# Nearest-neighbour upsampling: the second and third load issued behind the opening barrier and eight drains

## The chip, the cores and the metric

The kernel runs on one core of one Trainium2 chip. The metric is the device time of one execution in microseconds (us); of several executions, the median counts.

A core has five engines, each with its own queue of instructions: TensorE (PE), VectorE (DVE), ScalarE (ACT), GpSimd (POOL) and SyncE (SP). Data moves between the chip's main memory and the core's on-chip memory through 16 DMA engines. An engine that issues a transfer only hands it over, and goes on to its next instruction; the transfer itself runs on the DMA engines, and counts up a semaphore when it has landed.

## The reference

The input x has the shape (16, 64, 64, 64) in float32, 16.78 MB. Each element is written four times, so that height and width double; the output has the shape (16, 64, 128, 128), 67.11 MB.

```
for i in range(new_h):
    for j in range(new_w):
        src_i = i // scale_factor
        src_j = j // scale_factor
        result[:, :, i, j] = x[:, :, src_i, src_j].copy()
```

The scale factor is 2. There is no arithmetic: the kernel moves and repeats data.

## The kernel before, in words

**Tiling.** All rows of the input (16 x 64 x 64 of them, 64 elements each) are laid over the 128 partitions, 512 consecutive rows for each. So a partition's input is one run of 128 KB in main memory, and its output one run of 512 KB. The whole input fits on chip: one large on-chip tile holds it in `xt`, with free room ahead of it (lines 188 to 190).

**Loads.** Three loads bring the input in, cut by rows of a partition at `cuts = [0, 32, 288, 512]` (lines 194 to 197): the first has 32 rows (8 KB for each partition, 1 MB in all), the second 256 (64 KB, 8.4 MB), the third 224 (56 KB, 7.3 MB). All three are issued on SyncE's queue.

**Copies and stores.** The loop at line 206 goes over nine groups of rows, `[54, 38, 54, 60, 54, 62, 64, 62, 64]`. For each, VectorE copies the rows into their expanded form, every element twice and every row twice (line 217), and one store sends that to main memory (line 219). The expanded groups lie by turns in the free room ahead of `xt` and over input rows that have been used up. Group 0 is copied in two parts: its first row (line 216), which is in the first load, and its other 53 rows (line 217), which reach into the second load and wait for it. The stores 0, 1 and 8 are issued by SyncE, the others by ScalarE.

**What sets the order at the start.** The program has a first block, which ends in a barrier of all five engines, and a second block, the body, reached by a branch. In the barrier each engine executes a drain that counts up a gathering semaphore; GpSimd waits for all of them and then counts up the releasing semaphore, for which each engine waits. The barrier's instructions carry line 237 in the profile, the branch and the closing barrier line 251.

The loads stand in the body as it is built. `begin_before_barrier` (line 13) changes the finished program: it takes the first `EARLY` instructions of SyncE's body, which must be loads that wait for nothing, and puts them into the first block, ahead of SyncE's drain of the barrier. With `EARLY = 3` SyncE's queue therefore begins: load 1, load 2, load 3, drain, wait for the release, branch, and then the stores.

`close_early` (line 80) does something like it at the end, where GpSimd cleans up while the last store is in flight and SyncE waits for that store alone. The change doesn't touch it.

Of the kernel before, what the change touches and what calls it, by code (L numbers as in the profile page):

```python
# [6 lines left out]

EARLY = 3  # L10


def begin_before_barrier(nc):
# [5 lines left out]
    sp = mybir.EngineType.SP  # L19
    loads = [i for i in body.instructions if i.engine == sp][:EARLY]  # L20
    for load in loads:
# [132 lines left out]
@with_exitstack  # L154
def kernel(
    ctx: ExitStack,
    tc: tile.TileContext,
    x: bass.AP,
    scale_factor: int,
    out: bass.AP,  # L160
):
    nc = tc.nc
    nc.at_finalize(begin_before_barrier)
    nc.at_finalize(close_early)
    P = nc.NUM_PARTITIONS
    s = int(scale_factor)
    B, C, H, W = x.shape
    R = B * C * H // P
    fdt = x.dtype

    xp = x.rearrange("b c h w -> (b c h) w").rearrange("(p r) w -> p r w", p=P)
    op = out.rearrange("b c (h hd) w -> (b c h) (hd w)", hd=s).rearrange(
        "(p r) w -> p r w", p=P
    )

    rows = [54, 38, 54, 60, 54, 62, 64, 62, 64]
    GROW = s * s
    FREE = 79
    WF = FREE * GROW * W
    assert sum(rows) == R
    mem_pool = ctx.enter_context(tc.tile_pool(name="mem", bufs=1))
    LEAD = 32
    whole = mem_pool.tile([P, LEAD + WF + R * W], fdt, name="mem")
    mem = whole[:, LEAD:]
    xt = mem[:, WF:].rearrange("p (r w) -> p r w", r=R)  # L190

    HEAD = 32
    cuts = [0, HEAD, R // 2 + HEAD, R]
    for lo, hi in zip(cuts, cuts[1:]):
        nc.sync.dma_start(out=xt[:, lo:hi], in_=xp[:, lo:hi])  # L197

    def expanded(r0, r1):
        return (  # L200
            xt[:, r0:r1].unsqueeze(2).unsqueeze(4).to_broadcast([P, r1 - r0, s, W, s])
        )

    r0 = 0
    before = (0, 0)
    for n, k in enumerate(rows):
        size = k * GROW * W
        at = 0 if n % 2 == 0 else WF + r0 * W - size
        assert at >= before[1] or at + size <= before[0]
        before = (at, at + size)  # L210
        u = mem[:, at : at + size].rearrange(
            "p (k a w b) -> p k a w b", k=k, a=s, w=W
        )
        k0 = 1 if n == 0 else 0
        if k0:
            nc.vector.tensor_copy(out=u[:, :k0], in_=expanded(r0, r0 + k0))  # L216
        nc.vector.tensor_copy(out=u[:, k0:], in_=expanded(r0 + k0, r0 + k))  # L217
        issuer = nc.sync if n in (0, 1, len(rows) - 1) else nc.scalar
        issuer.dma_start(out=op[:, r0 : r0 + k, :], in_=u)
        r0 += k  # L220
# [35 lines left out]
```

## Time and profile before

| | |
|---|---|
| median of 3 runs | 197.26 us (197.02 to 197.47) |
| span of the profiled execution, first to last instruction | 195.8 us |
| what the median has beyond that span | 1.5 us |
| transfers | 12: 3 loads, 9 stores; 83.89 MB |
| mean rate over the span | 429 GB/s |
| VectorE busy | 76.9 us, 10 copies |

The page gives no time of the profiled execution beside its span; other executions of the kernel take the times of the first row.

How to read it: a profile's span runs from the first instruction to the last. Busy time is what an engine spends executing; register, branch, semaphore and transfer-issuing instructions don't count as busy. The "chain that ended last" follows the last piece of work back to what released it, step by step. "SPq" or "ACTq" in front of an operation means that the engine's queue issued or executed it without the engine counting as busy. The DMA row gives the mean busy share of the 16 DMA engines in 40 equal slices of a window, in tenths, with 9 for 90% or more. A packet is one run of bytes that one DMA engine moves; a transfer over 128 partitions has 128 of them here, and 16 small ones at its end that count up the semaphore. A packet's bytes are booked at one moment, so that short windows can show a rate or a share that is too high or too low.

### The profile page before, as it was taken

The numbers are of one execution on the slowest core, as the hardware profiler recorded it, in microseconds if no ns is written. First come the engines' busy times: TensorE is split into PE (matmuls) and PEld (weight loads), VectorE is DVE, ScalarE is ACT, GpSimd is POOL, SyncE is SP. The second block draws the span as 40 slices with busy tenths as digits, with TensorE's granted clock in tenths as the row PEclk, the third lists the DMA queues.
The fourth block names the chain that finished last, engine by engine and source line by source line (L and its number), as shares of the span: only waits on it lengthen the run. The fifth ranks groups of instructions, "written<-read, shape, count | busy, mean of one in ns | idle before, by whom it ended". The sixth has DMA issues, their size and how long they took to land.

```text
span 195.8 us, 76 instructions
## 1 busy us (share of the span) xinstructions
DVE 76.9 (39%) x10; POOL 0.2 (0%) x4
## 2 busy tenths in 40 slices
DVE  0000099990029287059008805920790079000000
POOL 0000000000000000000000000000000000000000
DMA  9999989989898988999999899999999999999994
GB/s 429 429 429 429 402 375 539 398 362 542 362 435 382 551 373 362 542 402 402 402 537 407 362 542 415 415 415 415 429 429 429 429 415 558 473 435 422 429 429 214
DMA packets 1728, 83.89 MB, mean 429 GB/s; under 512 B 192, under 2 KB 192, under 8 KB 192
## 3 DMA queue, kind: packets, MB, share of 16 engines
q10 hardware_dynamic: 864, 46.66, 55.0%
q1 hardware_dynamic: 864, 37.22, 44.2%
HBM read 16.78 MB, written 67.11 MB: 429 GB/s over the span
## 4 chain that ended last, share of the span: by engine, by line
DMA 61%; DVE 24%; SPq 0%; issue 0%
DMA out_dram<-mem 49%; DVE mem L217 24%; DMA mem<-in_x_dram 12%; SPq L197 0%
## 5 line engine op out<-in xcount | busy, mean ns | idle before, releaser
L217 DVE COPY mem<-mem 128x13824 f32<-128x13824 f32 (+5 forms) x9 | 76.6, 8515 | 84.6 <-DMA out_dram<-mem 65.6
L216 DVE COPY mem<-mem 128x256 f32<-128x256 f32 x1 | 0.3, 293 | 4.8 <-DMA mem<-in_x_dram 4.8
L237 POOL MEMSET const-bfloat16-1.0<- 128x1 bf16 x1 | 0.1, 102 | 0.0
L237 POOL MEMSET const-uint8-127<- 128x1 uint8 x1 | 0.1, 101 | 0.0
L237 POOL MEMSET const-float32-0.0<- 128x1 f32 x1 | 0.1, 98 | 0.2 <-issue 0.2
L237 POOL MEMSET const-float32-1.0<- 128x1 f32 x1 | 0.1, 98 | 0.0
## 6 DMA issues: line engine op xcount, KB each, us to landing
out_dram<-mem ACTq DMA_DIRECT2D x2, 7936.0 KB, 31.6
out_dram<-mem ACTq DMA_DIRECT2D x2, 6912.0 KB, 23.7
out_dram<-mem ACTq DMA_DIRECT2D x1, 7680.0 KB, 26.1
mem<-in_x_dram SPq DMA_DIRECT2D x1, 7168.0 KB, 40.2
out_dram<-mem SPq DMA_DIRECT2D x1, 6912.0 KB, 19.0
out_dram<-mem SPq DMA_DIRECT2D x1, 4864.0 KB, 25.2
mem<-in_x_dram SPq DMA_DIRECT2D x1, 1024.0 KB, 4.8
mem<-in_x_dram SPq DMA_DIRECT2D x1, 23.7
```

The source lines that it names most:

```text
L216: nc.vector.tensor_copy(out=u[:, :k0], in_=expanded(r0, r0 + k0))
L217: nc.vector.tensor_copy(out=u[:, k0:], in_=expanded(r0 + k0, r0 + k))
L237: nc = _bacc.Bacc("TRN2", target_bir_lowering=False, num_devices=1)
```

## The change

`EARLY` goes from 3 to 1, so that only the first load is put ahead of the barrier. In front of the second load SyncE gets eight drains that wait for nothing. SyncE's queue then begins: load 1, drain of the barrier, wait for the release, branch, eight drains, load 2, load 3, and then the stores as before. Copies, stores, their order and their engines stay as they are, and so do the sizes of the loads.

```diff
-EARLY = 3
+EARLY = 1
+PAUSES = 8
...
     cuts = [0, HEAD, R // 2 + HEAD, R]
-    for lo, hi in zip(cuts, cuts[1:]):
+    for n, (lo, hi) in enumerate(zip(cuts, cuts[1:])):
+        if n == 1:
+            for _ in range(PAUSES):
+                nc.sync.drain()
         nc.sync.dma_start(out=xt[:, lo:hi], in_=xp[:, lo:hi])
```

## The prediction

> **What bounds the kernel now.** I read the page first, for the span, the DMA row and the packet row; then the table of stretches, to see whether the transfer engines ever rest; then the chain of work, to see what the first microseconds wait for. The page:
>
> ```profile
> span 195.8 us, 76 instructions
> DVE 76.9 (39%) x10; POOL 0.2 (0%) x4
> DMA  9999989989898988999999899999999999999994
> HBM read 16.78 MB, written 67.11 MB: 429 GB/s over the span
> ```
>
> VectorE works 39% of the span, and the 16 DMA engines show 8 or 9 tenths in every slice but the last. The kernel is a stream of 16.78 + 67.11 = 83.89 MB. The stretches (columns: stretch and length, VectorE, GpSimd, clock, mean DMA share, GB/s) say it more sharply:
>
> ```profile
> 0.00:1.00 1.00, 0.00 (x0) 0.20 (x4) 1.00 0.00 0
> 1.00:2.00 1.00, 0.00 (x0) 0.00 (x0) 1.00 0.95 180
> 2.00:4.00 2.00, 0.00 (x0) 0.00 (x0) 1.00 0.98 414
> 4.00:195.40 191.40, 76.93 (x10) 0.00 (x0) 1.00 1.00 433
> 195.40:195.80 0.40, 0.00 (x0) 0.00 (x0) 1.00 0.00 0
> ```
>
> From 4.0 to 195.4 us the DMA share is 1.00 at 433 GB/s: 191.4 x 0.433 = 82.9 MB, all but 1.0 MB of the traffic. Nothing in that stretch can be made shorter by when a load is issued; it can only be moved as a block, or broken by a gap. So the whole question lies in the first 4 us: when the stream starts, and whether it runs on from the first load into the second. The chain of waits names the first links (start, length, what):
>
> ```profile
> 0.00 0.38 SPq L197
> 0.38 0.05 issue
> 0.43 23.65 DMA mem<-in_x_dram
> 24.09 0.02 issue
> 24.11 14.30 DVE mem L217
> 38.41 0.02 issue
> 38.42 19.01 DMA out_dram<-mem
> ```
>
> Load 1 takes SyncE 0.38 us, then 0.05 us pass, and load 2 is issued at 0.43 us. It lands at 24.09; the first large copy and the first large store hang on that. The chain calls load 2's transfer one piece of 23.65 us, but part of that is waiting behind load 1 in the same stream.
>
> When do the engines pass from load 1 to load 2? Load 1 has 128 rows of 8 KB and 16 small packets at the end, one for each engine. The packet rows of two windows, 0 to 4.02 us and then 4.02 to 4.5 us:
>
> ```profile
> DMA packets 125, 1.02 MB, mean 255 GB/s; under 512 B 0, under 2 KB 0, under 8 KB 0
> ...
> DMA packets 35, 1.07 MB, mean 2231 GB/s; under 512 B 16, under 2 KB 16, under 8 KB 16
> ```
>
> Before 4.02 us there are 125 of the 128 rows and no small packet; within the next 0.48 us come the last 3 rows, all 16 small packets, and 16 others, which carry 1.07 MB less 3 x 8 KB, that is 64 KB each: load 2's. So load 2's data is first needed at about 4.0 us, by the last engine at about 4.5. It was issued at 0.43 us. That is the slack of this change.
>
> **The change part by part.** No transfer is removed or resized, and no VectorE, ScalarE or GpSimd instruction changes place. SyncE's queue goes from load 1, load 2, load 3, barrier, branch, stores to load 1, barrier, branch, eight drains, load 2, load 3, stores. I work out when load 2 now issues. The instructions of the issuing and barrier lines (count, then ns as smallest/median/largest, then first and last start), come in three fences: the loads' line, the opening barrier's line, and line 251, which holds the branch and the closing barrier:
>
> ```profile
> L197 SPq DMA_DIRECT2D mem<-in_x_dram x3: 382/425/432, 0.0 to 0.9; - x3
> ```
>
> ```profile
> L237 POOLq DRAIN x1: 179/179/179, 0.3 to 0.3; - x1
> L237 PEldq DRAIN x1: 8/8/8, 0.3 to 0.3; - x1
> ...
> L237 SPq DRAIN x1: 125/125/125, 1.4 to 1.4; - x1
> L237 SPq EVENT_SEMAPHORE x1: 17/17/17, 1.7 to 1.7; - x1
> ...
> L237 PEldq EVENT_SEMAPHORE x1: 51/51/51, 1.7 to 1.7; - x1
> ```
>
> ```profile
> L251 PEldq DRAIN x2: 8/8/8, 1.8 to 167.3; - x2
> L251 ACTq DRAIN x2: 8/80/152, 147.3 to 167.2; - x2
> ...
> L251 SPq DRAIN x2: 7/68/129, 166.8 to 167.2; - x2
> ```
>
> *The barrier.* Now SyncE's own drain of the barrier starts at 1.4, behind three issues, and SyncE is through at 1.7: 0.3 us. GpSimd's drain ends at about 0.3 + 0.18 = 0.5 and TensorE's is at 0.3, so SyncE arrives last and will still do so: its drain moves to 0.43, right where load 2 was, and it is through at 0.43 + 0.3 = 0.73 us. The other engines are released about 1.0 us earlier; that is worth nothing, as VectorE's first copy idles 4.8 us for load 1's landing, and the first store waits for the copy that follows load 2:
>
> ```profile
> L216 DVE COPY mem<-mem 128x256 f32<-128x256 f32 x1 | 0.3, 293 | 4.8 <-DMA mem<-in_x_dram 4.8
> ```
>
> *The branch into the kernel's body.* SyncE's own cannot be seen now, with nothing timed behind it. TensorE passes its barrier wait at 1.7 and its next drain stands at 1.8, with a branch between: 0.1 us. So 0.83 us.
>
> *Eight drains.* A row of drains on SyncE is not in the trace. From below: the 7 ns of SyncE's idle drain and the 0.05 us step that lies between two of its instructions, 8 x 0.057 = 0.46 us. From above: the costliest drain of an idle queue, GpSimd's 179 ns, with the same step, 8 x 0.229 = 1.83 us; SyncE's own drain behind an issue (129 ns) gives 8 x 0.179 = 1.43. The drain of the barrier has already taken the part that lies behind load 1's issue, so the nearest row is the 7 ns one; I take 0.5 us. Load 2 issues at 0.83 + 0.5 = 1.3 us (bounds 1.3 to 2.7), load 3 one issue later (0.9 less 0.43 now, 0.47 us), at 1.8.
>
> The Trainium skill, page "VectorE: DVE Perf Modes", section "The DRAIN you can't avoid", says that the drains of a program's start and end take about 12 ns on all five engines. By it the eight would be 0.10 us, or 0.5 with the steps, an estimate from that page; the rows of 7 and 8 ns agree, those of 125, 129, 152 and 179 ns do not.
>
> *Does it arrive in time?* Load 1, issued at 0.0 into idle engines, shows no traffic before 1.0 us and a full rate from 2.0, so the price from issue to data lies between 1.0 and 2.0 us. Load 2's data can flow at 2.3 to 3.3 us; it is needed at 4.0. Slack 0.7 to 1.7 us: the rest of load 1's transfer covers the whole move, and without that cover each us would cost one us. Load 3 is needed only when load 2's 8.4 MB have passed, 20 us later; its move costs nothing. Behind the drains in SyncE's queue stand then only the stores, the first at 38.42, so the wait added holds up nobody else.
>
> Sum: 0 + 0 + 0 on a profiled span of 195.8 us. The median of the runs, 197.26, lies 1.5 us above that span; what lies around it is not touched. Forecast: **197.26 us**. A measurement of this kernel can tell about 0.2% (0.4 us) from no change.
>
> **The rivals.**
>
> *Load 2 comes too late (slower).* The one place is between 4.0 and 4.5 us, where each engine ends load 1. It decides from a load 2 issued later than 4.0 - 2.0 = 2.0 us if the slow end of the start-up applies, and 3.0 if the fast one does. With SyncE's 129 ns for each drain it issues at 0.83 + 1.43 = 2.26 and the gap is 0 to 0.26 us; with 179 ns it issues at 2.66 and the gap is 0 to 0.66 us. Counted at the top of these, the time is 197.5 to 197.9; its typical price, 0.5, gives 197.8. For it: four of the quoted drains take over 100 ns. Against it: all of those stand behind work of their own engine. Chance 0.19.
>
> The Trainium skill, page "DMA: Bandwidth & Descriptors", section "Latency and other measured facts", puts the latency of HBM at 0.2 us on average and 2 us at high load. Load 1 met idle engines, load 2 meets a busy stream, so by it load 2 needs up to 1.8 us more than the 1.0: an estimate of 1.3 + 1.0 + 1.8 = 4.1 us, a gap of 0.1. No row of before shows an issue with so little ahead of it.
>
> *The drains do more than that.* If a drain waited for load 1's landing, load 2 would be issued after 4.8 us; the engines would be empty from 4.0 to at least 4.8 + 0.5 + 1.0 = 6.3, and restart as slowly as at first: 2 to 3 us, about 199.8. Against it: SyncE's drain at 1.4 took 125 ns with three loads in flight and none landed. A stall at the branch of more than 2 us has the same effect. Chance 0.05.
>
> *The stream starts better (faster).* From 1.0 to 2.0 us the engines carry 180 GB/s, though their share is 0.95; at 433 this stretch would need 0.42 us. So 0.58 us are lost there. SyncE is issuing load 2 and load 3 from 0.43 to 1.33 us, and if it is their set-up that disturbs load 1's first packets, it leaves this stretch: at most 197.26 - 0.58 = 196.7, half of it 197.0. For it: the two coincide. Against it: the nine stores are issued into the running stream, between 38.42 us and SyncE's closing drain at 166.8, and the share there is 1.00 all the same; a start-up loss needs no second load to explain it. Chance 0.18.
>
> *The change doesn't do what it says.* The order of instructions shows load 2 and load 3 behind the branch, and the drains carry no wait; I give this nothing of its own beyond the second rival.
>
> **How the numbers follow.** Forecast (hidden, within 0.2%) 0.58; load 2 late 0.19, of which 0.14 costs more than 0.4 us; held up long 0.05; better start 0.18, of which 0.13 gains more than 0.4 us. Faster 0.13; slower 0.14 + 0.05 = 0.19; the same 0.58 + 0.05 + 0.05 = 0.68. The range goes from the full start-up gain, 196.7, to the upper gap, 197.9; only the long hold-up and the edges lie outside.
>
> **What would show it.** In the profile after: SyncE through the barrier at about 0.7 us; eight drains of some 10 ns at steps of 0.06 us; load 2 issued near 1.3 us and load 3 near 1.8; the 16 small packets of load 1 followed at once by 64 KB packets around 4.0 to 4.5 us; load 2 landing near 24.1 us; DMA share 1.00 behind 4 us; and 180 GB/s again from 1.0 to 2.0. Drains above 0.15 us, or a stretch without traffic between 4.0 and 5.5 us, would bear out the first rival; a rate well above 180 GB/s between 1.0 and 2.0 us and load 2 landing 0.3 us or more sooner, the third. The forecast is wrong if anything in the first 4 us shifts the landing of load 2 by more than 0.4 us.

## The result, and the profile after

The change makes the kernel slower: the median is 198.21 us (198.08 to 198.44, 5 runs) against 197.13 us (197.02 to 197.47, 5 runs), a ratio of 1.0048 with an interval of 1.0036 to 1.006, or 1.08 us. The forecast was 197.26, no change, with a range of 196.7 to 197.9. (It took the median of three runs of the kernel before; five runs give 197.13.)

The page of the changed kernel, the lines that answer to those of before:

```profile
span 196.8 us, 84 instructions
DVE 76.9 (39%) x10; POOL 0.2 (0%) x4
DMA  9999999999999999999999999999999999999994
HBM read 16.78 MB, written 67.11 MB: 426 GB/s over the span
```

The span is 1.0 us longer (195.8 before), with the same bytes and the same VectorE time. The stretches:

```profile
0.00:1.00 1.00, 0.00 (x0) 0.20 (x4) 1.00 0.03 8
1.00:2.00 1.00, 0.00 (x0) 0.00 (x0) 1.00 1.03 270
2.00:4.00 2.00, 0.00 (x0) 0.00 (x0) 1.00 1.60 647
4.00:195.40 191.40, 76.93 (x10) 0.00 (x0) 1.00 0.99 430
```

The short stretches mislead here: a packet counts whole where it starts, and some 64 KB packets of load 2 now start just ahead of 4.0 us, hence 647 GB/s. What counts is the start, where load 1 does a little better than before (270 for 180 GB/s), and the long stretch, whose share is 0.99 for 1.00. The chain of work:

```profile
0.71 0.05 issue
0.77 0.01 SPq L200
...
1.14 0.05 issue
1.19 23.99 DMA mem<-in_x_dram
25.18 0.02 issue
25.21 14.30 DVE mem L221
39.51 0.02 issue
39.52 18.95 DMA out_dram<-mem
```

Load 2 is issued at 1.19 and lands at 25.18 us, 1.10 later than before (24.08). Everything behind has its old length: the copy takes 14.30 us as before, the first store 18.95 for 19.01. So the loss is complete when load 2 has landed. SyncE's queue at the start, in the lines of the drains, the loads and the barrier:

```profile
L200 SPq DRAIN  x8: 7/7/7, 0.8 to 1.1; - x8
```

```profile
L201 SPq DMA_DIRECT2D mem<-in_x_dram x3: 333/372/425, 0.0 to 1.6; - x3
```

```profile
L241 SPq DRAIN x1: 131/131/131, 0.4 to 0.4; - x1
L241 SPq EVENT_SEMAPHORE x1: 17/17/17, 0.7 to 0.7; - x1
```

SyncE is through the barrier at 0.7 us, the drains take 7 ns each, and load 2 goes out a little earlier than forecast (1.19 for 1.3). Now the place where the engines pass from load 1 to load 2, in the packets that start in three windows, 3.7 to 4.3, 4.3 to 4.8 and 4.8 to 5.5 us:

```profile
DMA packets 36, 0.85 MB, mean 1420 GB/s; under 512 B 16, under 2 KB 16, under 8 KB 16
...
DMA packets 0, 0.00 MB, mean 0 GB/s; under 512 B 0, under 2 KB 0, under 8 KB 0
...
DMA packets 4, 0.26 MB, mean 374 GB/s; under 512 B 0, under 2 KB 0, under 8 KB 0
```

By 4.3 us all 16 engines have ended load 1 (16 small packets), and 12 have begun load 2: 0.85 MB is 12 packets of 64 KB and the last 8 rows of load 1. The other four begin load 2 only between 4.8 and 5.5 us. They were without work for 0.5 us at least, and the landing shows what it cost. Small packets of load 2, one for each engine as it ends, in the windows 23.3 to 24.25 and 24.25 to 25.4 us; before the change:

```profile
DMA packets 32, 0.92 MB, mean 966 GB/s; under 512 B 16, under 2 KB 16, under 8 KB 16
...
DMA packets 0, 0.00 MB, mean 0 GB/s; under 512 B 0, under 2 KB 0, under 8 KB 0
```

and after it:

```profile
DMA packets 22, 0.63 MB, mean 664 GB/s; under 512 B 11, under 2 KB 11, under 8 KB 11
...
DMA packets 10, 0.29 MB, mean 249 GB/s; under 512 B 5, under 2 KB 5, under 8 KB 5
```

Five engines end load 2 after 24.25 us, when all 16 had ended it before. That is one more than the four that began late, so the late beginnings are not the whole loss. The first packets of load 2 also take longer: by the time that the trace books for each packet, the 16 first ones take 2.74 us on the mean, against 2.42 before the change. The fifth engine began in time, at 4.26 us, but its first packet took 2.97 us and its second 2.54.

The delay is not made up later. The small packets of the last store after the change, in the windows 194.8 to 195.5 and 195.5 to 196.8 us:

```profile
DMA packets 8, 0.00 MB, mean 0 GB/s; under 512 B 8, under 2 KB 8, under 8 KB 8
...
DMA packets 8, 0.00 MB, mean 0 GB/s; under 512 B 8, under 2 KB 8, under 8 KB 8
```

Before, all 16 lay in the first of these windows. Put in order by the times at which they start and end, load 2's 128 packets fall into 16 chains of eight, in both kernels: the late engines move as many as the others, so the slowest one sets the end, and the time that is lost at 4.5 us is still missing at 196.

### The profile page after: what moved, and what is told of

Read it like the earlier page. It is cut to its first block, busy times and chain, and to the rows that moved or that the text cites. A ratio compares the mean times of both kernels' runs of the same rounds, so it can differ in the third digit from the quotient of the medians.

```text
span 196.8 us, 84 instructions
## 1 busy us (share of the span) xinstructions
DVE 76.9 (39%) x10; POOL 0.2 (0%) x4
## 2 busy tenths in 40 slices
DMA packets 1728, 83.89 MB, mean 426 GB/s; under 512 B 192, under 2 KB 192, under 8 KB 192
## 4 chain that ended last, share of the span: by engine, by line
DMA 61%; DVE 24%; issue 0%; SPq 0%
DMA out_dram<-mem 49%; DVE mem L221 24%; DMA mem<-in_x_dram 12%; SPq L200 0%
```

## The experiments

Theory A, from the result: load 2 now comes too late for some engines, by its moment of issue. Rivals: B, the drains or the barrier cost the time themselves; C, any load issued beside a running load loses a fixed time. Later names stand with their experiments.

### No drain behind the barrier (p0) and 24 of them (p24)

```diff
-PAUSES = 8
+PAUSES = 0     # p24: 24
```

> The changed kernel without its eight drains: load 1 ahead of the barrier, loads 2 and 3 behind it. Load 2 should issue at about 0.77 us, 0.42 earlier than the 1.19 of the changed kernel. Theory A (late by its moment of issue: four DMA engines get load 2's data some 3.6 to 4.2 us behind its issue, and wait for it): their gaps of 0.7 to 1.4 us shrink by 0.42, about 197.8 us. Theory B (the drains or the barrier themselves cost it): 197.1 if the drains do, 198.2 if the barrier does. Theory C (a load issued beside a running load loses a fixed time, whenever it is issued): 198.2.

> 24 drains in place of eight: load 2 at about 1.19 + 16 x 0.052 = 2.02 us. Theory A: all gaps grow by 0.83 us, about 199.0 us, and more than four engines wait. Theory B, by the drains: three times the loss of 1.1, about 200.3; by the barrier: 198.2. Theory C: 198.2.

p0 measured 197.22 us, ratio 1.0001 (0.9992 to 1.001): with the load at 0.78 us nothing is lost, though it is issued beside a running load, so C falls. p24 measured 197.71, 1.0032 (1.002 to 1.0045): with the load at 2.02 us there is *less* loss than at 1.19. The barrier and the branch are cleared (B in part), and so is a cost of each drain, which would have tripled. But A in its simple form, the later the worse, is missed as well.

### Only load 3 late (load3_late), all three ahead of the barrier with the drains between (drains_ahead)

```diff
-EARLY = 1
+EARLY = 2
...
-        if n == 1:
+        if n == 2:
```

> Loads 1 and 2 ahead of the barrier as before the change; only load 3 stands behind the barrier and the eight drains, at about 1.6 us. Theory A: load 3's data is needed only at about 23.7 us, so 197.1 us, as before. Theory B, by drains or barrier as such: 198.2. Theory C: load 3 is now the one issued beside a running load, so part of the loss comes back, 197.5 or more, with longer packets or idle engines near 2 to 7 us.

For the second, the function that moves the loads also takes drains, and `EARLY` counts 11 instructions (3 loads, 8 drains).

> All three loads ahead of the barrier, with the eight drains between load 1 and load 2; only the barrier's place differs from the changed kernel. Load 2 at about 0.43 + 8 x 0.052 = 0.85 us. Theory A: gaps 0.34 us shorter than in the changed kernel, about 197.85 us. Theory B, by the drains: 198.2; by the barrier: 197.1. Theory C: 198.2.

load3_late: 197.13 us, 0.9999 (0.999 to 1.0008); load 3, issued at 1.7 us with 20 us of cover, costs nothing, as A had it. drains_ahead: 197.12 us, 1.0 (0.9991 to 1.0009). Eight drains, and no loss: B by the drains falls. Load 2 stood at 0.98 us there, and A's 197.85 is missed too. So between 0.98 and 1.19 us something changes steeply.

### The same moment by another way (ahead12), its neighbours (p4, p12), and the changed kernel again (p8_again)

ahead12 has all loads ahead of the barrier and twelve drains between load 1 and 2; p4 and p12 have `PAUSES` 4 and 12.

> The changed kernel once more, beside its neighbours in drains. If the loss belongs to the program (its moment of issue), 198.2 us again and four engines that begin load 2 only at 4.8 us or later. If it belonged to one session of one chip, 197.1 and no such engines.

> All three loads ahead of the barrier, with twelve drains between load 1 and load 2: load 2 at 0.977 + 4 x 0.052 = 1.18 us, the moment that it has in the changed kernel (1.19), without barrier and branch in between. Theory D (the moment decides: about 1.2 us meets something that 0.98 and 2.02 do not): 198.2 us, four late engines. Theory E (the barrier and the branch between the loads decide, together with the drains): 197.1.

> Four drains behind the barrier: load 2 at 0.78 + 4 x 0.052 = 0.99 us, the moment it had in the kernel with eight drains ahead of the barrier (0.98, 197.12 us). Theory D: 197.1. Theory E: between 197.2 (no drain) and 198.2 (eight), about 197.7.

> Twelve drains behind the barrier: load 2 at 1.19 + 4 x 0.052 = 1.40 us. Theory D with a wide window (from 1.1 us on, until the start-up of load 1 is over near 2 us): 198.2 or more. Theory D with a narrow one: 197.1. Theory E: 198.2 or more, rising with the drains, which 24 drains (197.71) already speak against.

ahead12: 198.2 us, 1.0056 (1.0041 to 1.0071), load 2 at 1.18. p4: 197.06, 0.9999 (0.9989 to 1.0008), load 2 at 0.99. p12: 198.07, 1.0048 (1.0031 to 1.0065), load 2 at 1.41. The pair drains_ahead and ahead12 shares its place and differs in the moment; the pair p4 and drains_ahead shares its moment and differs in the place: the moment decides (D), the barrier and the branch do not (E falls). The number of drains doesn't either: eight lose nothing ahead of the barrier and 1.1 us behind it.

D's other forecast, four late engines, is missed. In ahead12 no packet starts between 4.8 and 5.5 us, so all 16 engines have begun load 2 by 4.8, the last at 4.58. Two of them end it late all the same; load 2's packets that start from 23.2 to 24.0 and from 24.0 to 25.0 us:

```profile
DMA packets 28, 0.80 MB, mean 1004 GB/s; under 512 B 14, under 2 KB 14, under 8 KB 14
...
DMA packets 4, 0.11 MB, mean 115 GB/s; under 512 B 2, under 2 KB 2, under 8 KB 2
```

The first packets of these two took 3.08 and 3.13 us, those of the others 2.42. Two slow engines cost as much here as five in the changed kernel.

p8_again: 198.25 us, 1.0051 (1.0036 to 1.0067), but two of its ten executions took 197.17 and 197.41. The profiled one is the first of these. Its packets that start from 4.3 to 4.8 and from 4.8 to 5.5 us:

```profile
DMA packets 19, 0.60 MB, mean 1196 GB/s; under 512 B 9, under 2 KB 9, under 8 KB 9
...
DMA packets 0, 0.00 MB, mean 0 GB/s; under 512 B 0, under 2 KB 0, under 8 KB 0
```

That is the same program without late engines and without the loss: every engine has taken up load 2 by 4.8 us, its first packets take 2.42 us, and load 2 lands at 24.27. With the same instructions at the same moments the loss occurs in most executions, not in all. The late beginnings alone are not its sign, as ahead12 shows: the engines that end load 2 late have either begun it late or taken longer for its first packet.

### More cover at the same moment (head52), and its control (head52_early)

```diff
-    HEAD = 32
+    HEAD = 52
```

> The changed kernel with a longer first load: cuts 0, 52, 308, 512 in place of 0, 32, 288, 512, so that load 1 runs to about 5.7 us and load 2, still issued at 1.19, has 1.5 us more cover. Theory H (the hand-over comes too late: load 2 reaches some engines only 3 to 4.3 us behind its issue): no gap is left, and the time is that of the control with all loads in front, about 197.1 us. Theory F (an issue between about 1.1 and 1.5 us into load 1's start disturbs the engines, whatever the cover): 198.1 again.

> The control for the longer first load: the same cuts 0, 52, 308, 512, all three loads ahead of the barrier as before the change. Both theories: as the kernel before, 197.1 us; anything else is what the cuts themselves do.

head52: 197.34 us, 1.0011 (1.0002 to 1.0021); its control with all loads in front: 197.36, 1.0012 (1.0003 to 1.0022). Load 2 was issued at 1.20, as in the changed kernel, and nothing was lost against the control. H's forecast is met, F falls: with more cover the same moment is harmless. The 0.25 us that both have over the kernel before belong to the cut.

### Load 2 alone (load3_later) and another queue (loads_on_scalar)

load3_later has 64 drains more between load 2 and load 3. In loads_on_scalar, ScalarE executes the eight drains and issues loads 2 and 3.

> Load 2 as in the changed kernel (eight drains, 1.19 us), but 64 drains more between load 2 and load 3, so that load 3 issues at about 1.53 + 64 x 0.052 = 4.9 us and not at 1.58. If load 2's moment alone decides (H or F): 198.2 us. Theory L (the two issues close together, load 3's set-up beside load 2's, make the late engines): 197.1.

> Loads 2 and 3 issued by ScalarE, behind the barrier and eight drains of its own, at about the same 1.2 us: load 2 no longer stands behind load 1 in one queue, the engines take turns between the two queues. Theory H, if the hand-over inside one queue is late: 197.1 us, and load 1 lands later than 4.6 us because load 2 runs beside it. Theory F (an issue into the running start disturbs, from whichever queue): 198.1.

load3_later: 198.22 us, 1.006 (1.004 to 1.008); load 3 at 5.0 us changes nothing, L falls. loads_on_scalar: 198.02, 1.0048 (1.0032 to 1.0064), by its time F's forecast. The engines did not take turns between the two queues, as was expected: load 2's packets start from 4.16 to 4.56 us, on each engine as load 1 ends there, and none of them takes longer than 2.42. The chain shows the loss in another place:

```profile
1.05 23.19 DMA mem<-in_x_dram
24.23 0.02 issue
24.26 14.30 DVE mem L222
38.56 0.02 issue
38.57 19.67 DMA out_dram<-mem
```

Load 2 went out at 1.05 us there, short of the 1.2 that was meant, and landed at 24.24, in time. The loss lies in the first store, 19.67 us for 19.01, where the engines pass from ScalarE's queue to SyncE's: all 16 begin it by 40.8 us, as before the change, but their first packets take 2.68 to 3.07 us, for 2.04. The run doesn't tell H and F apart.

### The curve of moments (p16, p24_b, p32, p48)

> Sixteen drains: load 2 at 1.61 us, a lead of about 2.5 us before load 1 ends. Theory H (the shorter the lead, the more is lost): 198.3 us or more. Theory W (a window of moments, while load 1's first packets are under way, from about 1.1 to 1.5 us): between 197.7 and 198.1, falling towards the value of 24 drains.

> Twenty-four drains once more, load 2 at 2.02 us. Theory W: 197.7 us again, and the profile shows load 2 begun on all 16 engines by 4.6 us. Theory H: late engines appear between 4.6 and 5.5 us in this profile, and the earlier one was the exception.

> Thirty-two drains: load 2 at 2.44 us, a lead of 1.6 to 2.0 us, as store 0 has before load 3's end in the kernel before, where nothing is lost. Theory W: 197.7 or less. Theory H: 198.5 or more.

> Forty-eight drains: load 2 at 3.27 us, a lead of 0.8 to 1.2 us, at or below the 1.0 to 2.0 us that load 1 needs from issue to full rate on idle engines. Both theories: a plain gap now, data at 4.3 to 5.3 us against 4.1 to 4.5 needed, 197.6 to 198.2 by the first rival of the prediction; under H with the late engines on top, 199 or more.

p16: 197.99 us, 1.0041 (1.0028 to 1.0054). p24_b: 197.94, 1.0041 (1.0027 to 1.0054), with executions anywhere from 197.26 to 198.48. p32: 197.24, 1.0008 (0.9999 to 1.0016). p48: 197.98, 1.0039 (1.0026 to 1.0052). In p48 it is no longer a few engines; its small packets of load 2 in the windows 23.3 to 24.25 and 24.25 to 25.4 us:

```profile
DMA packets 2, 0.06 MB, mean 60 GB/s; under 512 B 1, under 2 KB 1, under 8 KB 1
...
DMA packets 30, 0.86 MB, mean 748 GB/s; under 512 B 15, under 2 KB 15, under 8 KB 15
```

15 of 16 engines end load 2 late. Only in part is that the plain gap of the prediction's first rival, which it had from 3.0 us on: the engines end load 1 from 4.16 to 4.45 us, 12 have begun load 2 by 4.6 and the last begins at 5.23, but the first packets take 3.03 us on the mean, for 2.42. W describes the curve best, H's growing loss fails at p32. The profiled executions of p24 and p24_b landed load 2 in time (24.23 and 24.22 us); the second was the best of its eight, the first lost 0.5 of its 0.6 us behind that, in the chain's piece for the first store, 19.52 us for 19.01:

```profile
2.02 22.21 DMA mem<-in_x_dram
...
38.57 19.52 DMA out_dram<-mem
```

That piece holds the end of load 3, for which the store waits on each engine. Two packets of load 3, started at 38.62 and 38.67 us, just behind the issue of the store at 38.57, took 2.47 and 2.72 us for 2.12, and two engines ended load 3 only at 41.08 and 41.38 us; before the change the last ended at 40.76. What the other executions of p24_b lost, and where, no profile shows.

### What the moment is tied to (head52_p38, head16)

head52_p38 is head52 with 38 drains; head16 is the changed kernel with `HEAD = 16`.

> The longer first load (cuts 0, 52, 308, 512, end of load 1 at 5.5 to 5.9 us) with 38 drains: load 2 at about 0.78 + 38 x 0.052 = 2.76 us, 2.8 us ahead of load 1's end, the distance of the changed kernel. If the window is tied to the end of load 1 (a lead of 2.5 to 2.9 us is bad): about 198.3 us, against 197.35 of this cut's control. If it is tied to the start of load 1 (1.2 to 1.6 us): 197.35.

> The changed kernel with a shorter first load (cuts 0, 16, 272, 512): load 1 ends near 3.0 us, load 2 is still issued at 1.19, a lead of about 1.8 us as with 32 drains. If the window is tied to the start of load 1: about 198.2 us. If it is tied to the distance to its end: about 197.2.

head52_p38: 198.15 us, 1.0049 (1.0032 to 1.0066), 0.8 more than its control. The start of load 1 is long over at 2.75 us; what it shares with the changed kernel is the distance to load 1's end. Small packets of load 2 in the windows 24.9 to 25.7 and 25.7 to 26.5 us:

```profile
DMA packets 22, 0.57 MB, mean 718 GB/s; under 512 B 11, under 2 KB 11, under 8 KB 11
...
DMA packets 10, 0.26 MB, mean 326 GB/s; under 512 B 5, under 2 KB 5, under 8 KB 5
```

Again five engines end late; in the control no small packet lies in the second window. But here none began late. From 5.4 to 6.1 us the packets, and the share of 16 engines' time in that window that they take, are in the control (q1 is SyncE's queue)

```profile
DMA packets 35, 1.09 MB, mean 1555 GB/s; under 512 B 16, under 2 KB 16, under 8 KB 16
...
q1 hardware_dynamic: 35, 1.09, 360.1%
```

and in head52_p38

```profile
DMA packets 35, 1.09 MB, mean 1555 GB/s; under 512 B 16, under 2 KB 16, under 8 KB 16
...
q1 hardware_dynamic: 35, 1.09, 403.5%
```

These are the same 35 packets: the last three rows of load 1, its 16 small packets and the first packet of load 2 on each engine. They take 45.2 us of the engines' time and not 40.3 (403.5 and 360.1% of 16 x 0.7 us), so a first packet takes about 0.3 us more on the mean. The loss of this run is in packets that start in time and last longer.

head16: 200.13 us, 1.0147 (1.0131 to 1.0162), nearly three times the loss, where 197.2 or 198.2 was expected. Packets that start from 2.7 to 3.4, 3.4 to 4.4 and 4.4 to 5.8 us:

```profile
DMA packets 52, 0.82 MB, mean 1176 GB/s; under 512 B 16, under 2 KB 16, under 8 KB 41
...
DMA packets 0, 0.00 MB, mean 0 GB/s; under 512 B 0, under 2 KB 0, under 8 KB 0
...
DMA packets 15, 0.98 MB, mean 702 GB/s; under 512 B 0, under 2 KB 0, under 8 KB 0
```

11 engines begin load 2 by 3.4 us (0.82 MB is 11 packets of 64 KB and 25 of 4 KB); five have ended load 1 by 3.4 us and stand empty for a full us and more. The first packets take longer here too, 2.69 us on the mean. Load 2 lands at 25.41; with 0.52 MB less up to its end than in the kernel before, the rate before (433 GB/s) would put it at 22.9, an estimate, so 2.5 us are lost by then. Both forecasts are missed: the loss is not confined to distances of 2.5 to 2.9 us. How much of it the shorter first load costs by itself is not shown, as this cut has no control with all loads in front.

All kernels, by the distance from load 2's issue to the time when the first engines end load 1. That time is taken as 4.1 us for the old cut, 5.5 for cut 52 and 2.8 for cut 16; in single profiles it differs (3.75 us in the changed kernel's, which would make its distance 2.6). The landing is that of the profiled execution:

| kernel | load 2 issued | distance | load 2 landed | median us |
|---|---|---|---|---|
| head52 (control 197.36) | 1.20 | 4.3 | 25.52 | 197.34 |
| before | 0.43 | 3.7 | 24.08 | 197.13 |
| load3_late | 0.43 | 3.7 | 24.20 | 197.13 |
| p0 | 0.78 | 3.3 | 24.03 | 197.22 |
| drains_ahead | 0.98 | 3.1 | 24.23 | 197.12 |
| p4 | 0.99 | 3.1 | 24.09 | 197.06 |
| loads_on_scalar (loss in the first store) | 1.05 | 3.1 | 24.24 | 198.02 |
| ahead12 | 1.18 | 2.9 | 24.95 | 198.20 |
| changed kernel | 1.19 | 2.9 | 25.18 | 198.21 |
| p8_again (profiled execution: 197.17) | 1.19 | 2.9 | 24.27 | 198.25 |
| load3_later | 1.20 | 2.9 | 25.08 | 198.22 |
| head52_p38 (control 197.36) | 2.75 | 2.8 | 26.20 | 198.15 |
| p12 | 1.41 | 2.7 | 25.14 | 198.07 |
| p16 | 1.60 | 2.5 | 25.08 | 197.99 |
| p24, p24_b | 2.02, 2.04 | 2.1 | 24.23, 24.22 | 197.71, 197.94 |
| p32 | 2.43 | 1.7 | 24.20 | 197.24 |
| head16 | 1.19 | 1.6 | 25.41 | 200.13 |
| p48 | 3.26 | 0.8 | 25.04 | 197.98 |

With 3.1 us and more of cover nothing was lost at this place in any kernel; with 2.5 to 2.9 us it was 0.8 to 1.1 us in each of six, by the medians. Below that it is uneven: p32 and head16 have nearly the same cover and lie 2.9 us apart, with different first loads. The length of load 2's 16 first packets goes with the loss: 2.42 us on the mean in the profiles of the seven rows of 3.1 us and more and of p8_again, 2.44 to 2.53 in p24, p24_b and p32, and 2.50 (ahead12) to 3.05 (p12) in the other eight.

## Why the prediction was wrong, point by point

- **The bound: right.** The stream of 83.89 MB sets the time, and what happens behind the start only moves it: copy and store of the chain kept their lengths. "Without that cover each us would cost one us" holds too, but for the slowest engine: in ahead12 two of 16 that ended load 2 late were enough for the whole 1.1 us.
- **Barrier, branch, drains: right.** Load 2 issued at 1.19 us, 1.3 forecast; drains of 7 ns at steps of 0.05 us, as taken. The 12 ns that the Trainium skill, page "VectorE: DVE Perf Modes", section "The DRAIN you can't avoid", gives for the drains of a program's start and end is 5 ns more than these took.
- **"Does it arrive in time?": the step that failed.** It took the price from issue to data from load 1, which met idle engines: 1.0 to 2.0 us, hence data at 2.3 to 3.3 and a slack of 0.7 to 1.7 us. For a load issued behind a running one that was too low, and it left out that packets which have begun in time may take longer. In the changed kernel four engines showed no data until 4.8 to 5.5 us, 3.6 to 4.3 us behind the issue at 1.19, and the first packets of all 16 took 2.74 us on the mean for 2.42; load 2 landed 1.10 us late. The cover that was enough in every kernel tried is 3.1 us, not 2.0. The trace of before held no load issued with so short a lead behind another, only the first store, issued 1.9 us before load 3 ends without a loss; so the price was unknown, and the range for it should have reached well above the idle one.
- **Load 3: right.** Moved alone it costs nothing (197.13 us), and moving it further changes nothing (198.22).
- **First rival, "load 2 comes too late": the place was right, the condition wrong.** It was to decide from an issue at 2.0 to 3.0 us, with a price of up to 0.66. It decided between 0.99 and 1.18 us, at a price of 1.0. The plain gap that it described is there at 3.26 us only in part of the 0.85 us lost; the rest is longer first packets. The Trainium skill's rule beside it, page "DMA: Bandwidth & Descriptors", section "Latency and other measured facts", that HBM latency rises to 2 us at high load, pointed this way, but the estimate of 4.1 us from it was too early for those four engines, and no run shows that this latency is what held them up.
- **Second rival, drains that wait for the landing: wrong.** They took 7 ns each, and load 2 was issued at 1.19 us, long before load 1 landed at 4.6.
- **Third rival, a better start without loads 2 and 3 beside it: wrong as a cause.** The changed kernel's profile shows 270 GB/s from 1.0 to 2.0 us, but other executions with load 2 as late or later do not. The rows of p8_again and p24 for that stretch:

```profile
1.00:2.00 1.00, 0.00 (x0) 0.00 (x0) 1.00 1.01 156
```

```profile
1.00:2.00 1.00, 0.00 (x0) 0.00 (x0) 1.00 0.80 164
```

With load 2 issued at 2.02 us the start is as slow as before (180). The start-up loss needs no second load.

**What stays open.** It is shown that load 2's moment of issue causes the loss, and that a longer first load removes it at the same moment (head52) while a later issue brings it back (head52_p38). It is not shown why load 2, issued 2.5 to 2.9 us ahead of its turn, begins late on some engines and takes longer for its first packets on others, nor why p32 with 1.7 us escapes where head16 does not: the trace shows when packets start and end, not what passes between the queue and the engines. Nor is the distance a rule for every transfer: the first store of the kernel before is issued at 38.42 us, 1.9 us before the first engine ends load 3 (40.31), and all its packets take 2.04 us. That head16 halves the rows to 4 KB may matter; it wasn't tried by itself. No version beat both kernels: the best, p4, is at 0.9999 (0.9989 to 1.0008).

## What to carry to other kernels

The cover that a queued load needs is not the start-up of a load on idle engines. Where the stream is the bound, issue the second load early (here 3.1 us before the first one ended was enough in every kernel tried, and 2.9 was not), or make the first one longer. These distances hold for this kernel's second load; its first store did with 1.9 us. Look at each engine, not at the mean share: a delay on a few engines moves the mean by a hundredth and the end by its full length. Look at how long the packets take as well as when they start. And take a second profile of a kernel whose executions scatter: one execution of the same program can show no trace of the loss.

## What the runs showed of the hardware that was not expected

- In the changed kernel a load issued behind a running load of the same queue began on 12 engines as they became free (by 4.26 us), and on four others 3.6 to 4.3 us after its issue, where a load on idle engines showed data after 1.0 us.
- Packets can start in time and still cost the loss: in head52_p38 all 16 engines began load 2 by 6.0 us, as in its control, and its first packets took longer, up to 3.13 us for 2.42.
- The same program lost about 1 us in eight of ten executions and not in two (p8_again: 198.06 to 198.71, and 197.17 and 197.41; the 197.17 is the one that was profiled).
- With load 1 on SyncE's queue and load 2 on ScalarE's (loads_on_scalar), load 2 began on each engine only as load 1 ended there, 4.16 to 4.56 us, though it was issued at 1.05.
- Time can be lost around the passage from the last load to the first store as well: 0.66 us in loads_on_scalar, where the store's first packets took 2.68 to 3.07 us for 2.04, and 0.51 in p24, where two packets of load 3 took longer just behind the store's issue. Why it did so there and not in the kernel before wasn't tried.
